# A long single-core network kernel: background steps moved into the down projections, and the S5 outputs set two tiles behind the states

## The chip, the cores and the metric

One core of one Trainium2 chip runs the whole program in one launch. The metric is device time in microseconds (us), lower is better. A difference of 0.2% (4.9 us here) is about the least that a measurement of this kernel can tell from none.

## The reference

The network is two blocks of two layers on 512 tokens of width 1024, all in fp32. Cut to what matters here:

```python
def conv_glu_ffn(h, w_in, conv_w, conv_b, w_out):      # F = 2816, twice (ffn0, ffn1)
    u = h @ w_in
    up = jnp.pad(u, ((0, 0), (CONV_WIDTH - 1, 0), (0, 0)))
    u = sum(conv_w[k] * up[:, k:k + S] for k in range(CONV_WIDTH)) + conv_b
    gate, val = jnp.split(u, 2, axis=-1)
    return (jax.nn.gelu(gate, approximate=True) * val) @ w_out

def _s5_mixer(h, w_in, lam_re, ..., d, w_glu, b_glu):  # once (s5)
    u = (h @ w_in).astype(f32)
    ...                                                # a diagonal state space: 64 groups, 64 states,
    ...                                                # chunks, y = C x + d u
    y = jax.nn.gelu(y); return value * sigmoid(gate)   # of y @ w_glu + b_glu
```

The second block's layers are also scaled and shifted by vectors `silu(cond) @ ada_w + ada_b` (here: the "ada" products, a vector of 1024 times a matrix).

## The kernel before

**Stages.** The body runs pool, ffn0, attention, ffn1, s5, mlp0, ssd, mlp1 and a last norm one after the other; tokens lie on the free axis in two halves of 256. A product of fp32 matrices is three matmuls (`mm3`, L220 to L222): each operand is split in a high and a low part, high by high, low by high, high by low. Weights come in chunks of 512 KB (`wchunk`: a DMA on SP's queue, L192; ScalarE copies the high part, L205; VectorE subtracts the low part, L206). TensorE (PE) has four PSUM banks for products.

**The order.** The program writes the operations in some order, and a scheduler that comes with the tile framework turns this, before the launch, into one fixed queue for each engine. An engine takes its own queue strictly from the front; a row whose data isn't there holds back all rows behind it.

**An ffn layer** (`ffn_layer`, from L960) takes its 22 tiles of F in three phases: 8, 8 and 6. In a phase, each *pair* of tiles is a product of 96 matmuls into four banks (some 22 us), whose results VectorE reads at L969 (`u`, four rows for a pair; they make the banks free for the next pair) before the convolution (L975, L976), the gelu and the split (L321). After the phase, except the last, the *down projection* multiplies by `w_out`, 8 output tiles, each ended by `evac` (L1042). The last pairs' tail and the norm that follows are in `tail_` and the seam to the next layer.

**Background work.** `Background` holds generators; `bg[0](n)` takes n steps of each. It is called after each pair (with `rate`, L1039) and after each evacuation of a down projection (L1043, one step).

- In ffn0 the generator is `s5_tables`, about 72 steps that compute tables for the s5 stage, mostly on VectorE (L681 to L791) with small transposes on PE (L725, L784, L786). Whatever is left is emitted after the body.
- In ffn1 it is `s5_toeplitz` (16 steps: loads `tz`, ScalarE copies `th` at L805) and the ada products of `ada_units` (`vecmat`, L477 to L520), about 60 steps. These make 14 *blocks*. A block takes 8 loads of 256 KB (`as`, L495, two buffers, issued on POOL's queue), each multiplied and added on VectorE into `aa` (L498 for the first, L500 for the next seven; one buffer); ScalarE and VectorE split `aa` into three parts `ab` (L512, L514), and 12 matmuls of one column (`pn`, L484) sum over the partitions. VectorE reads `pn` at L487 (`sums`). One step is two loads, so a block is four steps. `due` puts a block's `pn` and `sums` behind the next block's second load.

**The s5 body** (L1466 to L1507) goes over 8 tiles. `states(n)`: PE forms `pv` (L1394) from the input U and table `vt`; ScalarE and VectorE rotate, scan and rotate back, and leave `xs`, whose first column POOL clears (L1407). `outputs(n)`: PE adds two products with table `ct` into `py` (L1416 from U, L1417 from `xs`; one bank), ScalarE copies it to `ys` and sends it through memory to be regrouped. `gelu(n)` reads that back (`yf`), makes `gh` (ScalarE) and `gl` (POOL, L1431). `glu_mm` multiplies these by `w_glu`. `tabs` and `ctabs` load tables on POOL's queue, 2 MB a tile. `project_u` makes the inputs of two tiles (48 products of mm3's kind); those of tiles 6 and 7 are made in iteration 1.

Of the kernel before, what the change touches and what calls it, by code (L numbers as in the profile page):

```python
# [21 lines left out]
P = 128  # L22
# [3 lines left out]
KD = D // P  # L26
# [36 lines left out]
def net_kernel(ctx: ExitStack, tc: tile.TileContext, I: dict, out: bass.AP, parts=ALL):  # L63
    nc = tc.nc
    V, A, G, T = nc.vector, nc.scalar, nc.gpsimd, nc.tensor
# [12 lines left out]
    def nm(s):  # L78
        uid[0] += 1
        return f"{s}_{uid[0]}"  # L80

    def at(s="a", dt=F32):
        return ap.tile([P, S], dt, tag="a", name=nm(s))
# [7 lines left out]
    def psmm():  # L91
        return psm.tile([P, 512], F32, tag="mm", name=nm("mm"))

    FULL = (0, S)
# [739 lines left out]
    bg = [no_bg]  # L834
# [125 lines left out]
    def ffn_layer(l, phases, late=None, rate=3):  # L960
        win, wout = I["ffn_w_in"][l], I["ffn_w_out"][l]
        S_ = {"ah": [], "al": [], "ft": [], "sq": Norm()}
        hd = Held([(win, 0, KD, c, 0, {}) for c in (0, F1)])
        nk = phases[-1][1] - phases[-1][0]
        tl = Held([(wout, phases[-1][0], nk, n * P, nk % 4, {}) for n in range(0, KD, 2)])

        def scaled(ps):
            u = tt("u")
            V.tensor_tensor(u, ps, S_["pre"].rs, ALU.mult)  # L969
            return u  # L970

        def conv(t, u, col):
            wv = lambda i: vc("ffn_conv_w", 3 * 44 * l + 44 * i + col)
            A.activation(t, u, AF.Identity, bias=vc("ffn_conv_b", 44 * l + col), scale=wv(2))
            V.scalar_tensor_tensor(t[:, 1:], u[:, :S - 1], wv(1), t[:, 1:], ALU.mult, ALU.add)  # L975
            V.scalar_tensor_tensor(t[:, 2:], u[:, :S - 2], wv(0), t[:, 2:], ALU.mult, ALU.add)  # L976

        def glu(j, ug, uv):
            tg, tv = tt("tg"), tt("tv")
            conv(tg, ug, j)  # L980
            A.activation(tg, tg, AF.Gelu_apprx_tanh)
            conv(tv, uv, JF + j)
            V.tensor_tensor(tv, tv, tg, ALU.mult)
            hi, lo = at("hi", F32R), at("lo", F32R)
            S_["split"], _ = split_to(hi, lo, tv, FULL)
            S_["ah"].append(hi)
            S_["al"].append(lo)

        def head(hf, pre):
            S_["pre"] = pre  # L990
            un = S_.setdefault("un", {})

            def evac(i, q, ps, span):
                if hf == 0:
                    un[i, q] = tt("un")
                V.tensor_tensor(un[i, q][:, slice(*span)], ps, pre.rs[:, slice(*span)], ALU.mult)
                if hf and i % 2:
                    glu(i - 1 + q, un.pop((i - 1, q)), un.pop((i, q)))

            hd.run(hf, pre.hi, pre.lo, evac)  # L1000

        def down(n, ps, span, first, last):
            ts = slice(*span)
            ft = S_["ft"]
            if first:
                ft.append(at("f"))
                A.activation(ft[n], ps, AF.Copy)
            else:
                V.tensor_tensor(ft[n][:, ts], ft[n][:, ts], ps, ALU.add)
                if last:  # L1010
                    S_["sq"].add(ft[n], span)

        def body_():
            hh, hl = S_["pre"].hi, S_["pre"].lo
            bg[0](2)
            for ph, (j0, j1) in enumerate(phases):
                final = ph == len(phases) - 1
                if final and late is not None:
                    late()
                for j in range(j0 if ph else 2, j1, 2):  # L1020
                    pp = {(i, q): psmm() for i in range(2) for q in range(2)}
                    src = [chunks(win, 0, KD, i * F1 + j * P) for i in range(2)]
                    if final and j == j1 - 2:
                        chs = [list(c) for c in src]
                        for q in range(2):
                            for i in range(2):
                                for ch in chs[i]:
                                    mm_chunk(pp[i, q], ch, q, hh, hl, KD, FULL)
                        for i in range(len(tl.runs)):
                            tl.load_apart(i)  # L1030
                    else:
                        for _ in range(2):
                            for i in range(2):
                                ch = next(src[i])
                                for q in range(2):
                                    mm_chunk(pp[i, q], ch, q, hh, hl, KD, FULL)
                    for q in range(2):
                        glu(j + q, *(scaled(pp[i, q]) for i in range(2)))
                    bg[0](rate)  # L1039
                if not final:  # L1040
                    def evac(n, ps, span):
                        down(n, ps, span, ph == 0, False)  # L1042
                        bg[0](1)  # L1043

                    project(wout, j0, j1 - j0, 0, (0, 8), S_["ah"], S_["al"], evac)
                    S_["ah"], S_["al"] = [], []

        def tail_(hf, nxt):
            if hf == 0:
                warm_sqrt(S_["split"].ins)  # L1050
            tl.run(hf, S_["ah"], S_["al"], lambda i, q, ps, span: down(2 * i + q, ps, span, False, True))

        return Layer(lambda nxt: PreScale(nxt, eps1, ("ffn_pre_g", 8 * l)), hd.load, head, body_, tail_,
                     lambda span, nxt, pre: post_add(S_["ft"], S_["sq"], "ffn_post_g", 8 * l, span, nxt, pre))

# [286 lines left out]
    def s5_layer(dr, pool, pa):  # L1342
# [43 lines left out]
        def states(n):  # L1386
            cs, sn = rot.pop(n)
            dec = tt("dec")
            G.tensor_copy(g3(dec), dr["r8"][:, 8 * n:8 * n + 8].unsqueeze(2).broadcast_to([P, 8, 64]))
            G.memset(g3(dec)[:, :, 0:1], 0.0)  # L1390
            pv = pa.tile([P, 512], F32, tag="pv", bufs=2, name=nm("pv"))
            for g in range(8):
                w = min(P, 512 - g * 64)
                S_["states"] = T.matmul(pv[:, g * 64:g * 64 + w], vt[n][g // 4][:, (g % 4) * P:(g % 4) * P + P],  # L1394
                                        U[n][:, g * 64:g * 64 + w], start=True, stop=True).ins
            vt.pop(n)
            sw, t1 = swapped(pv), tt("t1")
            V.tensor_tensor(t1, pv, cs, ALU.mult)
            V.tensor_tensor(sw, sw, sn, ALU.mult)
            V.tensor_tensor(t1, t1, sw, ALU.subtract)  # L1400
            st = tt("st")
            V.tensor_tensor_scan(st, dec, t1, 0.0, ALU.mult, ALU.add)
            sw = swapped(st)
            V.tensor_tensor(st, st, cs, ALU.mult)
            V.tensor_tensor(sw, sw, sn, ALU.mult)
            x_ = at("xs")
            G.memset(g3(x_)[:, :, 0:1], 0.0)  # L1407
            V.tensor_tensor(g3(x_)[:, :, 1:], g3(st)[:, :, :63], g3(sw)[:, :, :63], ALU.add)
            xs[n] = x_

# [54 lines left out]
        def body_():  # L1465
# [3 lines left out]
            def project_u(j):  # L1469
# [4 lines left out]
                for q in range(2):  # L1474
                    u_out(j + q, ps[q])

            for j in range(2 * S5_HEAD, KD - 2, 2):
                project_u(j)
            pp = None
            gk = 0  # L1480
            for n in range(KD + 2):
                if n == 1:
                    with tc.issue_after(S_["states"]):
                        project_u(KD - 2)
                    pp = [psmm() for _ in range(4)]
                if n == 2:
                    c0 = [list(chunks(wg, 0, KD, c)) for c in (0, D)]
                if n == 0:
                    stack = ExitStack()
                    for ins in S_["lastu"]:  # L1490
                        stack.enter_context(tc.issue_after(ins))
                if n < KD:
                    states(n)
                    tabs(n + 4)
                    ctabs(n + 1)
                if n == 0:
                    stack.close()
                if 0 <= n - 1 < KD:
                    outputs(n - 1)
                if 0 <= n - 2 < KD:  # L1500
                    gelu(n - 2)
                if n >= 5:
                    with tc.issue_after(S_["last"]):
                        glu_mm(pp, c0, range(gk, n - 4))
                    gk = n - 4
            S_["gk"] = gk
            S_["pp"], S_["c0"] = pp, c0  # L1507

# [461 lines left out]
    for name in names:  # L1970
# [20 lines left out]
            layer.body()  # L1991
            close("atc", "atps")
        elif name == "ffn1":
            layer = ffn_layer(1, ((0, 8), (8, 16), (16, 22)), rate=4)
            seam(prev, layer)
            if tables_due:
                start_tables()
# [75 lines left out]
```

## Time and profile before

| | |
|---|---|
| time, median of 3 runs | 2448.88 us (2448.77, 2448.88, 2451.74) |
| the profiled execution: its own time | 2448.6 us |
| its span, from first to last instruction | 2446.9 us |
| mean granted clock of TensorE | 0.974 of full speed |
| busy: PE / VectorE / ScalarE / POOL | 2303.6 / 1707.1 / 1139.7 / 419.4 us |
| ffn0, its seam to attention | about 36 to 490 us |
| ffn1, its seam to s5 | about 640 to 1130 us |
| s5 body | about 1141 to 1240 us |

Times within the trace are us from the span's start. PE is VectorE's customer and supplier at once: a stage is as fast as PE where PE never waits, and a wait of PE is a direct loss. "PEclk" is the share of the full 2.4 GHz that TensorE was granted, between 0.5 (1.2 GHz) and 1.

### The profile page before, as it was taken

The page shows a single profiled execution, that of the slowest core. Times are in us where ns is not written, and L with a number is a line of the kernel's source. Part 1 is how long each engine was busy: PE and PEld are TensorE (multiplying, and loading weights), DVE is VectorE, ACT ScalarE, POOL GpSimd, SP SyncE. Part 2 cuts the span into 40 slices and gives each one's busy share as a digit, 9 for nine tenths or more (in the row PEclk, how much of TensorE's full clock was granted, in tenths as well). Part 3 has the DMA queues.
Part 4 walks back from the last instruction along what each step waited for, and adds up shares of the span by engine and source line. Part 5 has one row for each costly group of instructions (what it writes and reads, how often), then busy time and mean ns, then how long its engine had stood idle before and what let it go on. Part 6 is the DMA issues. An engine that isn't in the chain of part 4 may idle for free.

```text
span 2446.9 us, 33813 instructions
## 1 busy us (share of the span) xinstructions
PE 2303.6 (94%) x12477; PEld 1948.5 (80%) x12477; DVE 1707.1 (70%) x3064; ACT 1139.7 (47%) x2030; POOL 419.4 (17%) x596
## 2 busy tenths in 40 slices
PE   6989998788989999988799999999999999999998
PEld 6778877775878888787779878789878878888888
DVE  6896979767778697886646666666777788533333
ACT  6533535466675343455534333344555554422322
POOL 2001120002431211110301011010242340200110
PEclk9999999889989999989899999999999999999999
DMA  4224453311465655455742555542333332233322
GB/s 123 81 91 137 145 152 118 106 59 45 127 193 174 195 179 190 159 198 170 220 141 73 172 164 189 186 151 74 113 95 99 108 101 89 91 95 98 100 82 74
DMA packets 265190, 315.52 MB, mean 129 GB/s; under 512 B 34161, under 2 KB 222401, under 8 KB 264001
## 3 DMA queue, kind: packets, MB, share of 16 engines
q1 hardware_dynamic: 220929, 233.64, 30.5%
q0 software_dynamic: 19648, 62.41, 8.1%
q10 hardware_dynamic: 24448, 17.31, 2.2%
q8 instruction: 98, 1.61, 0.3%
q14 instruction: 67, 0.55, 0.1%
HBM read 289.12 MB, written 24.18 MB: 128 GB/s over the span
## 4 chain that ended last, share of the span: by engine, by line
PE 63%; DVE 14%; DMA 10%; issue 7%; ACT 4%; POOL 1%; SPq 0%; ACTq 0%; DVEq 0%; POOLq 0%
PE mm L221 18%; PE mm L220 18%; PE mm L222 18%; DMA as<-in_ada_w 6%; DVE wl L206 3%; DVE aa L500 1%; ACT wh L205 1%; PE pb L1746 1%; PE mm L1676 1%; PE mm L1677 1%; PE mm L1678 1%; DMA tz<-d_k 1%; DVE u L969 1%; PE py L1417 1%; DVE aa L514 1%
## 5 line engine op out<-in xcount | busy, mean ns | idle before, releaser
L220 PE MATMUL mm<-h,wh 128*128 128x512 f32 (+1 forms) x1792 | 665.6, 373 | 31.9 <-ACT h L429 16.2
L221 PE MATMUL mm<-h,wh 128*128 128x512 f32 (+1 forms) x1792 | 666.7, 373 | 7.4 <-DVE h L430 3.7
L222 PE MATMUL mm<-h,wl 128*128 128x512 f32 (+1 forms) x1792 | 663.4, 371 | 0.2 <-DVE wl L206 0.2
L205 ACT ACTIVATE wh<-ws 128x1024 fp32r<-128x1024 f32 (+1 forms) x367 | 387.1, 1059 | 505.6 <-PE mm L221 427.6
L206 DVE TENSOR_TENSOR wl<-ws,wh 128x1024 fp32r<-128x1024 f32 (+1 forms) x367 | 462.3, 1262 | 210.9 <-ACT wh L205 204.5
L220 PEld LDWEIGHTS mm<-h,wh 128*128 128x128 f32 x1792 | 346.2, 194 | 90.5 <-ACT h L429 17.4
L221 PEld LDWEIGHTS mm<-h,wh 128*128 128x128 f32 x1792 | 347.0, 194 | 64.9 <-DVE h L398 5.7
L222 PEld LDWEIGHTS mm<-h,wl 128*128 128x128 f32 x1792 | 346.9, 194 | 55.6 <-issue 1.8
L220 PE MATMUL mm<-hi,wh 128*128 128x512 f32 (+1 forms) x1056 | 371.5, 356 | 10.4 <-ACT wh L205 10.0
L221 PE MATMUL mm<-lo,wh 128*128 128x512 f32 (+1 forms) x1056 | 372.5, 354 | 3.4 <-DVE lo L321 3.0
L222 PE MATMUL mm<-hi,wl 128*128 128x512 f32 (+1 forms) x1056 | 372.1, 354 | 3.1 <-DVE wl L206 3.1
L220 PEld LDWEIGHTS mm<-hi,wh 128*128 128x128 f32 x1056 | 202.0, 192 | 38.4 <-ACT wh L205 11.4
L221 PEld LDWEIGHTS mm<-lo,wh 128*128 128x128 f32 x1056 | 202.2, 191 | 30.4 <-DVE lo L321 4.8
L222 PEld LDWEIGHTS mm<-hi,wl 128*128 128x128 f32 x1056 | 201.8, 191 | 30.1 <-DVE wl L206 4.0
L500 DVE SCALAR_TENSOR_TENSOR aa<-as,cond,aa 128x512 f32<-128x512 f32 x168 | 131.0, 780 | 112.0 <-DMA as<-in_ada_w 110.9
L1298 POOL TENSOR_TENSOR r<-r 128x512 f32<-128x512 f32 x64 | 87.7, 1374 | 670.7 <-ACT r L1294 484.3
L512 ACT ACTIVATE ab<-aa 128x512 bf16<-128x512 f32 x78 | 51.7, 662 | 118.1 <-DVE aa L500 81.1
L321 DVE TENSOR_TENSOR lo<-r,hi 128x512 fp32r<-128x512 f32 x64 | 47.2, 743 | 76.7 <-ACT hi L319 76.6
L495 POOL DMA_DIRECT2D as<-in_ada_w x96 | 51.6, 538 | 241.7 <-DVE aa L500 120.7
L1319 DVE SCALAR_TENSOR_TENSOR x<-mm,mod,x 128x512 f32<-128x512 f32 (+1 forms) x76 | 48.9, 662 | 58.4 <-PE mm L222 58.3
L319 ACT ACTIVATE hi<-r 128x512 fp32r<-128x512 f32 x64 | 40.4, 631 | 71.1 <-POOL r L1298 71.0
L297 DVE TENSOR_TENSOR acc<-acc,sq 128x256 f32<-128x256 f32 (+1 forms) x148 | 62.5, 440 | 9.3 <-ACT sq L296 5.2
(507 smaller groups left out, 3669.0 us busy)
## 6 DMA issues: line engine op xcount, KB each, us to landing
ws<-in_mlp_w SPq DMA_DIRECT2D x124, 512.0 KB, 4.0
ws<-in_ffn_w_in SPq DMA_DIRECT2D x88, 512.0 KB, 4.4
as<-in_ada_w POOLq DMA_DIRECT2D x96, 256.0 KB, 3.2
as<-in_ada_w SPq DMA_DIRECT2D x96, 256.0 KB, 3.4
ws<-in_m_w_in SPq DMA_DIRECT2D x41, 512.0 KB, 3.7
ws<-in_ffn_w_out SPq DMA_DIRECT2D x40, 512.0 KB, 3.4
ws<-in_w_o SPq DMA_DIRECT2D x16, 512.0 KB, 3.9
ct<-d_tab POOLq DMA_DIRECT2D x8, 1024.0 KB, 5.7
```

Source lines behind the costliest of these rows:

```text
L205: A.activation(h_, s_, AF.Copy)
L206: V.tensor_tensor(l_, s_, f(h_), ALU.subtract)
L220: T.matmul(ps, wh, xh, start=first, stop=False)
L221: T.matmul(ps, wh, xl, start=False, stop=False)
L222: return T.matmul(ps, wl, xh, start=False, stop=last).ins
L297: V.tensor_tensor(dst, dst, sq[:, a:b], ALU.add)
L321: return hi_, V.tensor_tensor(lo[:, ts], src, f(hi[:, ts]), ALU.subtract)
L495: queue.dma_start(st, W[k * P:(k + 1) * P, cb * 512:(cb + 1) * 512])
L500: V.scalar_tensor_tensor(acc, st, col(k), acc, ALU.mult, ALU.add)
L512: A.activation(pv[j], av, AF.Copy)
L1298: G.tensor_tensor(r, r, r, ALU.mult)
L1319: V.scalar_tensor_tensor(xT[n][:, ts], ps, md(i, 5, n), xT[n][:, ts], ALU.mult, ALU.add)
```

## The change

In both ffn layers, no background step is taken after the last pair of the last phase, and two are taken at each evacuation of a down projection instead of one. In ffn1 the steps after a pair go from 4 to the default 3 (ffn0 keeps 5). In s5, the outputs run two tiles behind the states instead of one, the gelu three behind instead of two, the glu products start one iteration later; the inputs of tiles 6 and 7 are made in four pieces, one in each of the iterations 1 to 4; a tile's `ct` table is issued after the outputs before it; and `xs` is cleared before `pv` is formed.

```diff
             for q in range(2):
                 glu(j + q, *(scaled(pp[i, q]) for i in range(2)))
-            bg[0](rate)
+            if not (final and j == j1 - 2):
+                bg[0](rate)
         if not final:
             def evac(n, ps, span):
                 down(n, ps, span, ph == 0, False)
-                bg[0](1)
+                bg[0](2)
...
     G.memset(g3(dec)[:, :, 0:1], 0.0)
+    x_ = at("xs")
+    G.memset(g3(x_)[:, :, 0:1], 0.0)
     pv = pa.tile([P, 512], F32, tag="pv", bufs=2, name=nm("pv"))
...
-    x_ = at("xs")
-    G.memset(g3(x_)[:, :, 0:1], 0.0)
     V.tensor_tensor(g3(x_)[:, :, 1:], g3(st)[:, :, :63], g3(sw)[:, :, :63], ALU.add)
...
+    def project_steps(j):
+        ps = [psmm(), psmm()]
+        for i, ch in enumerate(last_w):
+            for q in range(2):
+                mm_chunk(ps[q], ch, q, hh, hl, KD, FULL)
+                if i:
+                    u_out(j + q, ps[q])
+                yield
...
-    for n in range(KD + 2):
+    for n in range(KD + 3):
         if n == 1:
+            last_w = list(chunks(win, 0, KD, (KD - 2) * P, perm=True))
+            last_u = project_steps(KD - 2)
+        if 1 <= n < 5:
             with tc.issue_after(S_["states"]):
-                project_u(KD - 2)
+                next(last_u, None)
+        if n == 5:
             pp = [psmm() for _ in range(4)]
...
             states(n)
             tabs(n + 4)
-            ctabs(n + 1)
...
-        if 0 <= n - 1 < KD:
-            outputs(n - 1)
         if 0 <= n - 2 < KD:
-            gelu(n - 2)
-        if n >= 5:
+            outputs(n - 2)
+        if n:
+            ctabs(n)
+        if 0 <= n - 3 < KD:
+            gelu(n - 3)
+        if n >= 6:
             with tc.issue_after(S_["last"]):
-                glu_mm(pp, c0, range(gk, n - 4))
-            gk = n - 4
+                glu_mm(pp, c0, range(gk, n - 5))
+            gk = n - 5
...
-    layer = ffn_layer(1, ((0, 8), (8, 16), (16, 22)), rate=4)
+    layer = ffn_layer(1, ((0, 8), (8, 16), (16, 22)))
```

The same instructions run; only their places differ. Three places in the engines' queues follow. The numbers behind names count buffers and differ between the two programs.

**Place 1, VectorE, in ffn1, around the first `u` (L969) of the second phase's first pair.** Before, the rows up to its second:

```order
L498 TENSOR_SCALAR aa_8391<-as_8389,cond 128x512
L500 SCALAR_TENSOR_TENSOR aa_8391<-as_8393,cond,aa_8391 128x512
L206 TENSOR_TENSOR wl_8640<-ws_8638,wh_8639 128x1024
L969 TENSOR_TENSOR u_8520<-mm_8396,rsx_7033 128x512
L500 SCALAR_TENSOR_TENSOR aa_8391<-as_8572,cond,aa_8391 128x512
L500 SCALAR_TENSOR_TENSOR aa_8391<-as_8575,cond,aa_8391 128x512
L206 TENSOR_TENSOR wl_8670<-ws_8668,wh_8669 128x1024
L500 SCALAR_TENSOR_TENSOR aa_8391<-as_8578,cond,aa_8391 128x512
L969 TENSOR_TENSOR u_8522<-mm_8398,rsx_7033 128x512
```

With the change:

```order
L498 TENSOR_SCALAR aa_8325<-as_8323,cond 128x512
L487 TENSOR_REDUCE sums_8343<-pn_8330 128x4
L500 SCALAR_TENSOR_TENSOR aa_8325<-as_8327,cond,aa_8325 128x512
L531 TENSOR_TENSOR mod<-sums_8343,vec 128x4
L500 SCALAR_TENSOR_TENSOR aa_8325<-as_8346,cond,aa_8325 128x512
L500 SCALAR_TENSOR_TENSOR aa_8325<-as_8349,cond,aa_8325 128x512
L500 SCALAR_TENSOR_TENSOR aa_8325<-as_8416,cond,aa_8325 128x512
L500 SCALAR_TENSOR_TENSOR aa_8325<-as_8419,cond,aa_8325 128x512
L500 SCALAR_TENSOR_TENSOR aa_8325<-as_8422,cond,aa_8325 128x512
L500 SCALAR_TENSOR_TENSOR aa_8325<-as_8425,cond,aa_8325 128x512
L969 TENSOR_TENSOR u_8590<-mm_8466,rsx_7033 128x512
L969 TENSOR_TENSOR u_8592<-mm_8468,rsx_7033 128x512
```

The pair's first `u` now stands behind all eight loads of the block `aa_8325`, and behind `sums` of the block before it; before, it stood behind two loads of its block. Between the last `u` of the phase before and this one there are now 33 loads (L498 and L500), before 24. At the same place of the third phase there are 35, before 23, and there too all eight loads of a block and a `sums` stand ahead of the `u`.

**Place 2, PE, the same moment: the last rows ahead of the second pair's first matmul (L220).** Before:

```order
L484 LDWEIGHTS ab_8383
L484 MATMUL pn_8556<-one_86,ab_8383 128x1
L484 LDWEIGHTS ab_8383
L484 MATMUL pn_8556<-one_86,ab_8383 128x1
L220 MATMUL mm_8604<-h_6596,wh_8609 128x512
L221 MATMUL mm_8604<-h_6597,wh_8609 128x512
```

With the change:

```order
L484 LDWEIGHTS ab_8317
L484 MATMUL pn_8330<-one_86,ab_8317 128x1
L484 LDWEIGHTS ab_8430
L484 MATMUL pn_8444<-one_86,ab_8430 128x1
L484 LDWEIGHTS ab_8430
L484 MATMUL pn_8444<-one_86,ab_8430 128x1
L484 LDWEIGHTS ab_8430
L484 MATMUL pn_8444<-one_86,ab_8430 128x1
L484 LDWEIGHTS ab_8430
L484 MATMUL pn_8444<-one_86,ab_8430 128x1
L220 MATMUL mm_8652<-h_6596,wh_8657 128x512
L221 MATMUL mm_8652<-h_6597,wh_8657 128x512
```

Before, twelve `pn` matmuls stood between the two pairs, all of the block `aa_8211`, which was finished in the rows ahead. Now there are sixteen: the twelve of `pn_8330`, which place 1's `sums` waits for and which stand behind the whole first pair, and four on `ab_8430`, which is made from `aa_8325` when its eighth load has been added. `mm_8652` needs the bank that the first `u` frees.

**Place 3, POOL, in s5, around the first `gl` (L1431 before, L1432 with the change).** `xs_11482` before is tile 3's, and so is `xs_11407` with the change. Before:

```order
L1361 DMA ct_11493<-d_tab 128x2048
L1389 COPY dec_11522<-r_103 128x512
L1390 MEMSET dec_11522 128x8
L1431 TENSOR_TENSOR gl_11453<-yf_11449,gh_11452 128x512
L1407 MEMSET xs_11482 128x8
L1353 DMA vt_11485<-d_tab 128x512
```

With the change:

```order
L1393 MEMSET xs_11407 128x8
L1354 DMA vt_11433<-d_tab 128x512
L1354 DMA vt_11434<-d_tab 128x512
L1391 MEMSET dec_11489 128x8
L1362 DMA ct_11538<-d_tab 128x2048
L1390 COPY dec_11551<-r_103 128x512
L1432 TENSOR_TENSOR gl_11467<-yf_11463,gh_11466 128x512
L1391 MEMSET dec_11551 128x8
L1393 MEMSET xs_11492 128x8
```

Tile 3's clearing moves from behind the first `gl` to ahead of it; tile 4's (`xs_11492`) is now the first one behind it.

## Rows read from the trace of the kernel before

**Rows 1.** The page, part 1: busy time, share of the span, instructions.

```profile
PE 2303.6 (94%) x12477; PEld 1948.5 (80%) x12477; DVE 1707.1 (70%) x3064; ACT 1139.7 (47%) x2030; POOL 419.4 (17%) x596
```

**Rows 2.** The chain that ended last, 780 to 1090 us: its shares by line.

```profile
by line: DMA as<-in_ada_w 29.3%; issue 25.3%; DVE aa L500 6.9%; DVE wl L206 6.5%; DVE u L969 3.0%; PE mm L221 2.7%; ACT wh L205 2.6%; DVE tg L975 2.4%; PE mm L222 2.3%; PE mm L220 2.2%; DVE aa L514 1.9%; DVE tv L975 1.9%; POOL as L495 1.6%;
```

**Rows 3.** VectorE in order of time: start, duration, line, operation [idle before, releaser].

```profile
790.70 0.68 DVE L969 TENSOR_TENSOR u<-mm,rsx 128x512 f32<-128x512 f32 x1
...
810.60 0.49 DVE L498 TENSOR_SCALAR aa<-as,cond 128x512 f32<-128x512 f32 x1 [0.70 <-ACT ab L512]
...
838.88 0.75 DVE L500 SCALAR_TENSOR_TENSOR aa<-as,cond,aa 128x512 f32<-128x512 f32 x1 [2.26 <-DMA as<-in_ada_w]
...
843.10 0.75 DVE L500 SCALAR_TENSOR_TENSOR aa<-as,cond,aa 128x512 f32<-128x512 f32 x1 [1.67 <-DMA as<-in_ada_w]
...
850.74 0.49 DVE L498 TENSOR_SCALAR aa<-as,cond 128x512 f32<-128x512 f32 x1 [0.70 <-ACT ab L512]
...
853.07 0.68 DVE L969 TENSOR_TENSOR u<-mm,rsx 128x512 f32<-128x512 f32 x1
```

**Rows 4.** The same view, start of the third phase.

```profile
926.99 0.68 DVE L969 TENSOR_TENSOR u<-mm,rsx 128x512 f32<-128x512 f32 x1
...
948.47 0.47 DVE L498 TENSOR_SCALAR aa<-as,cond 128x512 f32<-128x512 f32 x1
...
991.83 0.49 DVE L498 TENSOR_SCALAR aa<-as,cond 128x512 f32<-128x512 f32 x1 [0.70 <-ACT ab L512]
```

**Rows 5.** TensorE in order of time: a wait in ffn0, two ends of first pairs.

```profile
137.95 0.77 PE L220 MATMUL mm<-h,wh 128*128 128x512 f32 x1 [6.06 <-DVE u L969]
...
857.02 0.45 PE L484 MATMUL pn<-one,ab 128*128 128x1 bf16 x12
...
991.22 0.35 PE L484 MATMUL pn<-one,ab 128*128 128x1 bf16 x8
```

**Rows 6.** DMA issues: count, KB each, median us from issue to landing.

```profile
as<-in_ada_w POOLq DMA_DIRECT2D x96, 256.0 KB, 3.2
```

**Rows 7.** Groups by line, VectorE, 30 to 475 us: first and last of 20 table lines.

```profile
L763 DVE TENSOR_TENSOR ct<-b,s5v 128x512 f32<-128x512 f32 x16 | 11.0, 685 | 0.1
...
L689 DVE MEMSET s5z<- 128x128 f32 x1 | 0.2, 165 | 0.0
```

**Rows 8.** Stretches: PE, PEld, DVE, ACT, POOL busy (instructions), PEclk, DMA share, GB/s.

```profile
138.00:148.00 10.00, 10.00 (x36) 8.08 (x37) 10.00 (x27) 5.29 (x8) 0.00 (x0) 0.80 0.01 2
190.00:230.00 40.00, 40.00 (x195) 32.62 (x194) 20.59 (x33) 13.21 (x18) 6.00 (x10) 1.00 0.43 132
340.00:370.00 30.00, 30.00 (x142) 24.25 (x141) 17.30 (x31) 7.73 (x10) 5.97 (x40) 1.00 0.47 145
410.00:440.00 30.00, 20.34 (x119) 16.51 (x117) 29.77 (x53) 14.96 (x23) 3.46 (x6) 0.77 0.57 179
1030.00:1050.00 20.00, 14.62 (x79) 12.54 (x78) 19.14 (x26) 11.65 (x16) 1.61 (x3) 0.83 0.66 218
1160.00:1220.00 60.00, 47.42 (x319) 44.56 (x318) 39.81 (x47) 30.91 (x46) 19.29 (x36) 0.89 0.74 233
```

**Rows 9.** Waits of TensorE, 1070 to 1130 us: total, times, longest.

```profile
PE mm L220 <- ACT h L429: 6.1, 2, 4.2
PE pn L314 <- DVE dg L311: 4.0, 2, 3.0
...
PE pn L484 <- ACT ab L512: 1.2, 2, 0.7
```

**Rows 10.** The same view, the s5 body, 1141 to 1240 us.

```profile
PE py L1417 <- DVE xs L1408: 5.6, 3, 4.0
PE py L1417 <- POOL xs L1407: 2.5, 1, 2.5
PE py L1416 <- ACT ys L1420: 2.4, 2, 1.7
...
PE pv L1394 <- DVE t L1398: 1.9, 1, 1.9
```

## The prediction, made blind

> **What bounds the kernel now.** I read the page first: PE is busy 94% of the span, VectorE 70% [rows 1]. So only two things can change the time by much: waits of PE, and stretches in which it runs below full clock. I then listed PE's waits by stretch, the clock in the same stretches, and last the chain that ended last, to see who is late. Two stretches lose to VectorE's table work and the clock that falls after it (410 to 440), to the end of the ada steps (1030 to 1050); s5 loses in a string of waits [rows 8, 10]. But the chain of waits says something that PE's own waits do not: from 780 to 1090 the largest part of the chain that ended last, 29%, is the landing of `as` loads, and VectorE's adding of them is the next work on it [rows 2]. PE hardly waits there, but the row of loads has no slack. The change puts more of them into that stretch.
>
> **The pace of the loads.** `as` has two buffers, so a load waits until VectorE has finished with the load two before it. From 810.60 to 850.74, through the down projection, VectorE went through two blocks, 16 loads: 40.14 / 16 = 2.51 us a load, and stood idle for the DMA between them [rows 3]. In the third phase two blocks took 948.47 to 991.83: 2.71 us a load [rows 4]. The quickest two in succession came 4.22 us apart, 2.11 each [rows 3].
>
> **ffn1: what is added.** Eight evacuations ask for 2 steps of 2 loads each, 32 loads in a down projection and more with the pairs. VectorE's queue keeps that order: between the last `u` of the first phase and the first `u` of the second there are now 33 loads, before 24. From 790.70, 33 x 2.51 = 82.8 us end at 873.5. PE ends the first pair at 857.0 [rows 3, 5], and cannot begin the second: it needs that `u` for the bank, and has `pn` matmuls of the unfinished block ahead in its own queue. It waits **16 us**. Before, the `u` came at 853.07, in time. At the third phase there are 35 loads: from 926.99, 87.9 us end at 1014.8, and the pair ends at 991.2 [rows 4, 5]: **24 us**, both shifted alike by the first wait. Behind the `u` on VectorE stand the convolution and the weights' low parts; PE stands, so they cost nothing beyond that. The pairs after it have 8 loads or fewer each, 20 us in a pair of 22: no further wait.
>
> Bounds. At 2.71 us a load the waits are 23 and 31. At 2.11 the sum of loads gives 3 and 10, but a second rule of the order holds then: `sums` ahead of the last seven loads needs `pn` matmuls that stand behind the whole first pair. Of those seven, two lie in the buffers; five at 2.11 and two additions of 0.75 [rows 3] make 12 us after the pair's end, at each place. So 24 to 54, and I take 40, from the pace of the down projection that these loads run in.
>
> One rule of the skill would make it less. The median landing of these loads is 3.2 us for 256 KB [rows 6]. The Trainium skill (DMA: Bandwidth & Descriptors, section Anatomy of one DMA — SWDGE (gpsimd) path) gives 2.0 us plus the bytes at 436 GB/s for a load of this kind, an estimate of 2.6 us here; with two in flight that takes 0.3 us off the pace of 2.51, and the waits would be 12 and 13 instead of 16 and 24. The trace shows the longer landing, beside the weight loads of the same stretch, and no run here shows the shorter; the sum goes by the trace.
>
> **The clock after a wait.** After a wait of 6.06 us in ffn0, the next 10 us, in which PE was busy throughout, were granted 0.80 [rows 5, 8]: 2 us lost. Two waits, 2 us each: **4 us**; at most 3 each, since 1030 to 1050 with its waits lost 0.17 x 14.6 = 2.5 us [rows 8].
>
> **ffn0: what is moved.** 120 us of table work on VectorE [rows 7] over some 72 steps are 1.67 us a step. The 8 extra steps in each down projection are 13.3 us, put where VectorE was free 19.4 of 40 us (190 to 230) and 12.7 of 30 (340 to 370) [rows 8]: no wait of PE. These steps are VectorE's own work with few loads, so they have no pace but VectorE's. At the end, 9 steps fewer (10 for 15 and 4 leftovers) take 15 us off VectorE where it is busy 29.77 of 30 us; PE lost there 30 - 20.3 = 9.7 us waiting and 0.23 x 20.3 = 4.7 us by the clock, 14.4 in all [rows 8]. Some of it is weights that land late, so I take **-11**, between -4 (the work merely moves to the start of a phase) and -14.
>
> **ffn1's end and the seam.** No ada step is left there. 1030 to 1050 lost 5.4 us waiting and 2.5 by the clock [rows 8]: -8. In the seam the waits on `ab` (1.2), on `h` (6.1) and on `dg` (4.0) [rows 9] stand in part behind the last block's splits on ScalarE and VectorE; they also exist in a seam without such work, so -6 of 11. Together **-14**, between -5 and -19. The last block's loads leave POOL's queue to the s5 tables there; that is in it.
>
> **s5.** The same work with one tile more between states and outputs, and the last input products cut in four, so that a tile's `pv` can come between them; that moves work on PE and saves none. Waits on `xs`, its clearing, `ys` and `t`: 12.4 us, and the clock 0.11 x 47.4 = 5.2: 17.6 at most [rows 10, 8]. Sure is the clearing, 2.5, which no longer stands behind `gl`. The rest hangs on whether the chain of a tile on ScalarE and VectorE, or the transfers (0.74 of the DMA engines over 60 us [rows 8]), set the pace anyway; the loads that read tiles 6 and 7 back now come later too, behind a `yf` on SP's queue. **-6**, between 0 and -18.
>
> **The sum**, on the profiled execution's 2448.6 (its span is 2446.9; the median of the runs, 2448.88, is 0.3 above): 40 + 4 - 11 - 14 - 6 = +13, so **2462 us**. What counts as no change is 0.2%, 4.9 us.
>
> **Rivals.**
> - *The loads come quickly* (the other side). The mechanism is the pace of `as`: the waits are 68p - 130.6 for a pace p, and with the clock they equal the gains of 31 at p = 2.32. Below that the floor of 24 holds: 24 + 4 - 31 = -3, 2446; with gains of 40, 2437. For it: VectorE waits for the DMA, not for work, and two loads came at 2.11. Against: no whole block ran below 2.5.
> - *The gains don't come* (s5 stays bound by its transfers and a tile's chain, table work comes back at the start of ffn0's phases): gains of 9, so 2484; with the pace of 2.71 as well 2497. For it: the DMA share in s5, and VectorE nearly full in ffn0.
> - *All gains come in full*, the waits as forecast: 44 - 51 = -7, 2442. Against: it needs every clock loss to go.
>
> **How the numbers follow.** The forecast, waits of 35 to 54 with gains of 20 to 35, has 0.62: 2452 to 2475 or so, slower. The second rival has 0.16, slower. The first has 0.17, a little more than half of it within 4.9 us of before; the third 0.05, faster. Faster 0.12, the same 0.13, slower 0.75. The range of 2444 to 2482 leaves a tenth on either side.
>
> **What would show it.** In the changed profile: two waits of PE of over 10 us, just after the first pair of ffn1's second and third phases (near 857 and, shifted, 1007), put down to `ab` or `u`, with a granted clock below 1 behind each; VectorE idle on `as` there; 410 to 440 and the end of ffn1 free of waits over 1 us; no wait on POOL's clearing in s5. It is wrong if PE goes from pair to pair there without a stop, or if the waits are under 10 us, and then 68p - 130.6 has failed.

## The result, and the profile after

| | before | changed |
|---|---|---|
| time, median | 2450.31 us (4 runs, 2448.77 to 2456.92) | 2475.85 us (4 runs, 2473.06 to 2481.46) |
| ratio of the times | | 1.0102, 95% interval 1.0076 to 1.0128 |
| the profiled execution: its own time, span | 2448.6, 2446.9 | 2476.7, 2475.0 |
| mean granted clock | 0.974 | 0.969 |

Slower by 25.5 us, 1.0%. Forecast was 2462, in a range of 2444 to 2482. PE does the same work:

```profile
PE 2300.2 (93%) x12477; PEld 1942.5 (78%) x12477; DVE 1714.8 (69%) x3064; ACT 1142.9 (46%) x2030; POOL 418.4 (17%) x596
```

PE's 2300.2 us answer to the 2303.6 of before [rows 1]; the added time is waiting. To see where, four moments that both traces have: PE's first matmul of attention's part that waits for `kr`, a norm's product at the start of ffn1, the first input product of s5, and s5's first product behind `sgm`. The changed kernel, TensorE in order of time:

```profile
496.89 0.80 PE L220 MATMUL mm<-h,wh 128*128 128x512 f32 x1 [2.44 <-DVE kr L1113]
...
694.44 0.68 PE L314 MATMUL pn<-dg,ones 128*128 128x128 f32 x4 [0.89 <-DVE dg L311]
...
1152.44 0.79 PE L220 MATMUL mm<-h,wh 128*128 128x512 f32 x1 [2.54 <-DVE us L1370]
...
1265.05 0.50 PE L220 MATMUL mm<-gh,wh 128*128 128x512 f32 x1 [2.02 <-ACT sgm L1460]
```

And the kernel before (the numbers in brackets are the idle time just before a row and what ended it):

```profile
521.97 0.79 PE L220 MATMUL mm<-h,wh 128*128 128x512 f32 x1 [2.44 <-DVE kr L1112]
...
720.76 1.19 PE L314 MATMUL pn<-dg,ones 128*128 128x128 f32 x4 [4.70 <-DVE dg L311]
...
1128.79 0.79 PE L220 MATMUL mm<-h,wh 128*128 128x512 f32 x1 [2.01 <-DVE us L1369]
...
1239.87 0.50 PE L220 MATMUL mm<-gh,wh 128*128 128x512 f32 x1 [2.00 <-ACT sgm L1459]
```

Attention is reached **25.1 us earlier** (496.89 for 521.97), ffn1 26.3 earlier, s5's first product **23.7 later**, so ffn1 costs **+50.0**; s5 ends 25.2 later (+1.5), and the span ends 28.1 later (some 3 us in the stages behind, in small pieces). So the small loss is the difference of a gain and a loss that are both large. (Such a moment differs by a few us between executions: three kernels whose ffn0 is as before reach the `kr` wait at 521.97, 523.86 and 526.10.)

The two waits are there. TensorE's waits from 826 to 856 us, the start of the second phase:

```profile
PE pn L484 <- ACT ab L512: 21.2, 4, 16.1
```

and from 975 to 1020, the start of the third (0.7 us more stand earlier, in the pair):

```profile
PE pn L484 <- ACT ab L512: 26.7, 7, 14.9
```

VectorE in order of time shows what they wait for:

```profile
764.79 0.68 DVE L969 TENSOR_TENSOR u<-mm,rsx 128x512 f32<-128x512 f32 x1
...
835.28 0.48 DVE L498 TENSOR_SCALAR aa<-as,cond 128x512 f32<-128x512 f32 x1
835.67 0.16 DVE L487 TENSOR_REDUCE sums<-pn 128x4 f32<-128x12 f32 x1
...
839.68 0.75 DVE L500 SCALAR_TENSOR_TENSOR aa<-as,cond,aa 128x512 f32<-128x512 f32 x1 [3.06 <-DMA as<-in_ada_w]
...
849.56 0.75 DVE L500 SCALAR_TENSOR_TENSOR aa<-as,cond,aa 128x512 f32<-128x512 f32 x1 [0.66 <-DMA as<-in_ada_w]
850.23 1.28 DVE L969 TENSOR_TENSOR u<-mm,rsx 128x512 f32<-128x512 f32 x2
...
924.78 0.68 DVE L969 TENSOR_TENSOR u<-mm,rsx 128x512 f32<-128x512 f32 x1
...
1016.45 1.28 DVE L969 TENSOR_TENSOR u<-mm,rsx 128x512 f32<-128x512 f32 x2
```

From the first phase's last `u` (764.79) to the next one (850.23) VectorE spent 85.4 us on 33 loads, 2.59 us each, and from 924.78 to 1016.45 91.7 us on 35, 2.62 each. In front of many loads it stands idle for the landing, 3.06 us in the longest case shown. PE had ended the first pair's product at 829.0 and the third phase's first pair at 993.2. These rows answer to [rows 3, 4].

The changed kernel by stretches (columns as in [rows 8]):

```profile
410.00:450.00 40.00, 39.01 (x272) 36.28 (x271) 27.46 (x50) 19.21 (x34) 0.00 (x0) 1.00 0.35 105
450.00:500.00 50.00, 41.27 (x305) 39.47 (x305) 44.04 (x122) 31.41 (x82) 0.00 (x0) 0.91 0.26 80
831.50:851.50 20.00, 1.25 (x17) 1.00 (x18) 9.56 (x16) 3.52 (x6) 4.73 (x9) 0.52 0.45 145
852.00:862.00 10.00, 10.00 (x43) 7.68 (x43) 9.61 (x18) 5.25 (x8) 1.07 (x2) 0.79 0.16 50
1018.00:1028.00 10.00, 10.00 (x39) 7.68 (x40) 9.92 (x17) 6.04 (x9) 0.54 (x1) 0.73 0.15 47
```

The first two rows are ffn0's end and the seam behind it: 39.0 of 40 us busy at full clock in the first. The third is the wait, PE busy 1.25 of 20 us; the fourth and fifth are the 10 us behind each wait, at 0.79 and 0.73, PE busy throughout: 2.1 and 2.7 us lost.

In s5 PE's waits on `xs` and its clearing [rows 10] are gone, and one on `ys` has come. Waits of TensorE, 1164 to 1270 us:

```profile
PE py L1417 <- ACT ys L1421: 15.0, 5, 5.3
```

### The profile page after: what moved, and what is told of

Read it like the earlier page. It is cut to its first block, busy times and chain, and to the rows that moved or that the text cites. A ratio compares the mean times of both kernels' runs of the same rounds, so it can differ in the third digit from the quotient of the medians.

```text
span 2475.0 us, 33840 instructions
## 1 busy us (share of the span) xinstructions
PE 2300.2 (93%) x12477; PEld 1942.5 (78%) x12477; DVE 1714.8 (69%) x3064; ACT 1142.9 (46%) x2030; POOL 418.4 (17%) x596
## 4 chain that ended last, share of the span: by engine, by line
PE 43%; DVE 5%; DMA 2%; ACT 1%; issue 1%; DVEq 0%; ACTq 0%
PE mm L221 12%; PE mm L220 12%; PE mm L222 12%; DMA as<-in_ada_w 2%; DVE wl L206 1%; PE pb L1762 1%; PE mm L1692 1%; PE mm L1693 1%; PE mm L1694 1%; DVE aa L500 0%; ACT wh L205 0%; DVE u L394 0%; PE pb L1768 0%; DMA ws<-in_mlp_w 0%; PE py L1417 0%
## 5 line engine op out<-in xcount | busy, mean ns | idle before, releaser
L220 PE MATMUL mm<-h,wh 128*128 128x512 f32 (+1 forms) x1792 | 665.0, 373 | 23.5 <-ACT h L429 7.3
L220 PEld LDWEIGHTS mm<-h,wh 128*128 128x128 f32 x1792 | 344.7, 193 | 81.6 <-issue 8.8
L220 PE MATMUL mm<-hi,wh 128*128 128x512 f32 (+1 forms) x1056 | 369.1, 354 | 6.8 <-ACT wh L205 6.1
L220 PEld LDWEIGHTS mm<-hi,wh 128*128 128x128 f32 x1056 | 200.7, 190 | 34.2 <-ACT wh L205 6.8
L500 DVE SCALAR_TENSOR_TENSOR aa<-as,cond,aa 128x512 f32<-128x512 f32 x168 | 130.9, 779 | 132.3 <-DMA as<-in_ada_w 131.1
L495 POOL DMA_DIRECT2D as<-in_ada_w x96 | 51.6, 538 | 252.5 <-DVE aa L500 120.2
```

The lines of the kernel that those rows point to most:

```text
L220: T.matmul(ps, wh, xh, start=first, stop=False)
L495: queue.dma_start(st, W[k * P:(k + 1) * P, cb * 512:(cb + 1) * 512])
L500: V.scalar_tensor_tensor(acc, st, col(k), acc, ALU.mult, ALU.add)
```

## The experiments

**The three parts by themselves.** Each edit alone in the kernel before. A ratio is always to the kernel before as measured beside the run; its median was 2452.05, 2450.65 or 2448.18 us, so runs that stand far apart below are best compared by their ratios. First ffn0:

```diff
-                    bg[0](rate)
+                    if not (l == 0 and final and j == j1 - 2):
+                        bg[0](rate)
...
-                        bg[0](1)
+                        bg[0](1 if l else 2)
```

> The kernel before with the change in ffn0 alone: two table steps at each evacuation, none after the last pair; ffn1 and s5 as before. Theory (the change gains 25 us in ffn0 and its seam and loses 50 in ffn1): the trace of the changed kernel reaches attention's first product 25 us earlier, so 2424 us, with everything behind it moved by the same 25. Rival (the earlier start only moves a wait into attention or ffn1, and the gain is given back there): 2440 or above.

Measured: 2427.58 us (before: 2452.05), ratio 0.9900, interval 0.9877 to 0.9923. The theory holds: 24.5 us, and no more of it is given back behind than the runs' spread. The stretches of this run:

```profile
410.00:450.00 40.00, 38.77 (x261) 35.60 (x260) 28.50 (x50) 20.25 (x35) 0.00 (x0) 1.00 0.31 99
450.00:500.00 50.00, 41.21 (x322) 39.84 (x320) 42.31 (x121) 29.06 (x77) 0.00 (x0) 0.94 0.25 79
```

and the same of the kernel before, to the wait for `kr` (at 499.87 above, at 521.97 here):

```profile
410.00:450.00 40.00, 28.50 (x183) 24.32 (x182) 35.47 (x65) 18.62 (x29) 5.33 (x9) 0.83 0.51 165
450.00:522.10 72.10, 57.07 (x423) 54.38 (x421) 51.17 (x142) 36.46 (x96) 0.45 (x2) 0.87 0.22 68
```

Idle time is 11.5 + 15.0 us before, 1.2 + 8.8 now: 16.5 less. The half clock cost 0.17 x 28.5 + 0.13 x 57.1 = 12.3 us before, 0.06 x 41.2 = 2.5 now: 9.8 less. So more than a third of what went is clock, and half of the clock's part lies in the seam, behind 450. (The two make 26.3, more than the 22.1 us by which this trace reaches `kr` earlier: at 410 the two programs are not at quite the same work. The shares are rough.)

Then ffn1 alone (two steps at an evacuation and none after the last pair where `l` is 1, `rate` 3):

```diff
-                    bg[0](rate)
+                    if not (l == 1 and final and j == j1 - 2):
+                        bg[0](rate)
...
-                        bg[0](1)
+                        bg[0](2 if l else 1)
...
-            layer = ffn_layer(1, ((0, 8), (8, 16), (16, 22)), rate=4)
+            layer = ffn_layer(1, ((0, 8), (8, 16), (16, 22)))
```

> The kernel before with the change in ffn1 alone: two ada steps at each evacuation, three after a pair, none after the last. Theory (two waits behind the as loads, 21 and 27 us, and 5 us of half clock, little gained at the end): 2449 + 50 = 2499 us, two waits of over 15 us each in the phases' first pairs. Rival (part of the two waits came from attention ending earlier, so that loads and weights collided): under 2485.

Measured: 2503.61, ratio 1.0219, interval 1.0200 to 1.0237: 51.6 us slower. Waits of TensorE in this run, 856 to 886 us, and then 1005 to 1050:

```profile
PE pn L484 <- ACT ab L512: 21.0, 4, 15.7
```

```profile
PE pn L484 <- ACT ab L512: 26.3, 6, 15.4
```

They have the size that they have in the whole change, so they owe nothing to attention's earlier end. And s5 alone, the s5 part of the diff, of which this is a piece:

```diff
-            for n in range(KD + 2):
+            for n in range(KD + 3):
...
-                if 0 <= n - 1 < KD:
-                    outputs(n - 1)
...
+                    outputs(n - 2)
...
```

> The kernel before with the change in s5 alone. Theory (the waits on xs and its clearing go, waits of the same size on ys come in their place, since py has one bank and its copy stands on ScalarE behind the state chain of the tile in work): 2450, within 4 us of before. Rival (what I forecast: the waits go by half): 2443.

Measured: 2450.73, ratio 1.0003, interval 0.9992 to 1.0013: no difference. The waits of TensorE in its s5 body, 1141 to 1242 us, where before there were 12.4 us [rows 10]:

```profile
PE py L1416 <- ACT ys L1420: 14.1, 4, 7.1
```

One wait has taken the other's place. The three parts add up: -24.5 + 51.6 - 1.3 = +25.8, and the whole change measured +25.5.

**What sets the pace of the loads.** The whole change, with more `as` buffers; `tz` gives up one, to make room:

```diff
-                st = pool.tile([P, 512], F32, tag="as", bufs=2, name=nm("as"))
+                st = pool.tile([P, 512], F32, tag="as", bufs=4, name=nm("as"))
...
-            tz = pool.tile([P, 8, P], F32, tag="tz", bufs=2, name=nm("tz"))
+            tz = pool.tile([P, 8, P], F32, tag="tz", bufs=1, name=nm("tz"))
```

> The whole change with four as buffers instead of two, and one tz buffer instead of two to make room. Theory (the pace of 2.5 us a load is the round trip of two buffers, landing plus VectorE plus issue): four in flight bring the pace toward 1.3 us, 33 loads end in time, both waits fall under 5 us and the time to about 2430. Rival (the pace is set by the issuing engine or by the bandwidth beside the weight loads): the two waits stay over 15 us each, and the time at 2470 to 2480.

Measured: 2423.95, ratio 0.9891, interval 0.9873 to 0.9909: 51.9 us under the whole change. Both waits are gone (the view lists no wait of TensorE from 780 to 1010). VectorE in this run, the first rows of two blocks with two blocks' loads from one to the other:

```profile
794.02 0.48 DVE L498 TENSOR_SCALAR aa<-as,cond 128x512 f32<-128x512 f32 x1
...
819.91 0.49 DVE L498 TENSOR_SCALAR aa<-as,cond 128x512 f32<-128x512 f32 x1 [0.70 <-ACT ab L512]
```

25.9 us for 16 loads, 1.62 each, for 2.51 [rows 3], though a load takes longer to land than the 3.2 us of before [rows 6]:

```profile
as<-in_ada_w POOLq DMA_DIRECT2D x96, 256.0 KB, 3.6
```

Three buffers, the same edit with `bufs=3`:

> The whole change with three as buffers and one tz buffer. Theory (the pace is the round trip divided by the buffers): 5.0 us by 3 is 1.7 us a load, 32 loads take 54 us where PE gives 66, so both waits are gone, or nearly, and the time is that of four buffers, 2424 to 2432. Rival (a fixed time per load sets it): waits of 10 us or more stay.

Measured: 2427.75, ratio 0.9904, interval 0.9885 to 0.9924. Of the two waits 2.7 and 3.6 us are left. The same two rows:

```profile
797.05 0.49 DVE L498 TENSOR_SCALAR aa<-as,cond 128x512 f32<-128x512 f32 x1 [0.70 <-ACT ab L512]
...
828.59 0.49 DVE L498 TENSOR_SCALAR aa<-as,cond 128x512 f32<-128x512 f32 x1 [0.70 <-ACT ab L512]
```

1.97 us a load. So 2, 3 and 4 buffers give 2.51, 1.97 and 1.62: the buffers in flight set the pace, but less than in proportion (pace times buffers is 5.0, 5.9, 6.5 us). The landing grows a little, and the waits for it run out: of the two blocks' time VectorE waited 14.2 us for landings with two buffers, 7.6 with three and 2.1 with four, where it was busy for 19.0 of the 25.9 us. With four, VectorE's own work and the splits at a block's end are most of the pace. Nor are three buffers as good as four, though the medians differ by 3.8 us only: in the profiled executions ffn1, from its first product to s5's, takes 432.9 us with three and 419.9 with four. The control, one `tz` buffer with two of `as`:

> The whole change with one tz buffer and as as it is, two. It tells what the smaller tz alone does in the runs with more as buffers. Theory: nothing that matters, 2470 to 2480 with the two waits of 21 and 27 us. Rival (part of the gain with four buffers came from tz): under 2460.

Measured: 2475.38 in one run, with waits of 22.3 and 24.4 us on `ab`. The smaller `tz` does nothing that one run can tell.

**Fewer steps in ffn1's down projections.** The whole change (three steps after a pair, none after the last), with

```diff
-                        bg[0](2)
+                        bg[0](1 if l else 2)
```

> The whole change, but in ffn1 one ada step at each evacuation as before (three after a pair, none after the last). Theory (the two steps make the lateness; with one there are 23 loads in each stretch and no wait, but three blocks are left for the end and the seam): no wait over 2 us at the phases' starts, 5 to 15 us lost at the seam, 2430 to 2440. Rival (the waits come from the place of sums and pn behind the pair, not from the number of loads): waits of 10 us stay.

Measured: 2460.18, ratio 1.0038, interval 1.0023 to 1.0054. The first half of the theory holds: PE waits 0.2 us in all for a `u`, and for no `ab`, at the phases' starts, with 23 loads ahead of each first `u`. The time is 20 us over what I expected. Three blocks are left for the end, and PE waits for them there, from 1045 to 1092 us:

```profile
PE pn L484 <- ACT ab L512: 36.1, 6, 15.0
```

36.1 us, on the last two of the three: what is left over does not slip in between the seam's work, it stands ahead of it in PE's queue in one heap, at the pace of two buffers. The loads' lateness can be put in two places, but with two buffers this edit does not schedule it away. The kernel before does, with four steps after every pair, the last too: there PE waits 2.4 us for `ab` in all of ffn1.

**What holds s5.** In the changed kernel ScalarE shows why `ys` is late (ScalarE in order of time):

```profile
1210.63 0.59 ACT L1384 ACTIVATE sw<-pv 64x512 f32<-64x512 f32 x1
1215.81 0.63 ACT L1383 ACTIVATE sw<-st 64x512 f32<-64x512 f32 x1 [4.59 <-DVE st L1405]
1216.45 0.63 ACT L1384 ACTIVATE sw<-st 64x512 f32<-64x512 f32 x1
1217.11 0.60 ACT L1421 ACTIVATE ys<-py 128x512 f32<-128x512 f32 x1
```

The copy of `py` to `ys`, which frees the one `py` bank, stands behind the two swaps of the next tile's state, and in every tile these wait for VectorE's scan, 4.59 us here and 30.2 us in the eight tiles. An edit on the kernel with four `as` buffers takes the outputs between the scan and the swaps:

```diff
             V.tensor_tensor_scan(st, dec, t1, 0.0, ALU.mult, ALU.add)
+            if n >= 2:
+                outputs(n - 2)
             sw = swapped(st)
...
-                if 0 <= n - 2 < KD:
+                if KD <= n < KD + 2:
                     outputs(n - 2)
```

> The kernel with four as buffers, and in s5 the outputs of two tiles back taken between the scan and the rotation back, so that the copy of py to ys stands on ScalarE ahead of the two swaps that wait for the scan. Theory (s5 gains nothing because that copy waits behind the scan of another tile, 4 us a tile, and py has one bank): the five waits on ys, 15 us in all, fall under 5, and the time drops by 8 to 12 from 2424, to 2412 to 2416. Rival (s5 is bound by its table transfers or a tile's chain on VectorE): PE waits as long for something else, and the time stays within 4 us of 2424.

Measured: **2409.09 us**, ratio 0.9828, interval 0.9812 to 0.9845, 14.9 under the run without the edit (15.4 by the ratios), more than expected. TensorE's waits in its s5 body, 1110 to 1212 us:

```profile
PE py L1419 <- ACT ys L1423: 5.0, 2, 3.3
PE mm L220 <- ACT sgm L1462: 2.0, 1, 2.0
PE py L1420 <- POOL xs L1393: 1.1, 1, 1.1
```

15 us on `ys` have become 5.0. Is the two tiles' distance needed for it? The same kernel, with outputs one tile behind again:

```diff
-            if n >= 2:
-                outputs(n - 2)
+            if n >= 1:
+                outputs(n - 1)
...
-                if n:
-                    ctabs(n)
-                if 0 <= n - 3 < KD:
-                    gelu(n - 3)
-                if n >= 6:
+                ctabs(n + 1)
+                if 0 <= n - 2 < KD:
+                    gelu(n - 2)
+                if n >= 5:
...
```

> The kernel of the run with four as buffers and the early copy of py, but with the outputs one tile behind the states again, the gelu two behind and the glu products one iteration earlier, as before the change; the input products stay in four pieces. Theory (what s5 needs is the copy ahead of the swaps, and the second tile of distance is what lets py be formed while the scan of the next tile runs, with nothing waiting on xs): waits on xs come back, 5 us or more, and the time is 4 to 10 above 2409. Rival (the distance is worth nothing once the copy comes early): within 3 us of 2409.

Measured: 2421.5, ratio 0.9891, interval 0.9874 to 0.9908: 12.4 above (15.4 by the ratios). Waits in its s5 body, 1110 to 1225 us:

```profile
PE py L1420 <- DVE xs L1411: 12.2, 6, 3.1
```

So the distance takes the wait off `xs`, and the earlier copy takes it off `ys`; each alone only changes the name of the wait. The length of s5 in the traces, from its first input product to the product behind `sgm`, says the same: 110.3 to 111.1 us in the three kernels with s5 as before, 109.2 to 113.6 in the five with the change as it is, 112.9 here with the early copy but one tile's distance, and 100.4 with both.

**ffn1 as before, with the rest.** The early copy and the change in ffn0 and s5; ffn1 with two buffers, one step, `rate` 4:

```diff
-                    if not (final and j == j1 - 2):
+                    if not (l == 0 and final and j == j1 - 2):
...
-                        bg[0](2)
+                        bg[0](1 if l else 2)
...
-            layer = ffn_layer(1, ((0, 8), (8, 16), (16, 22)))
+            layer = ffn_layer(1, ((0, 8), (8, 16), (16, 22)), rate=4)
```

> The change in ffn0 and in s5 with the early copy of py; ffn1 as before, with two as buffers, one ada step at an evacuation, four after a pair. Theory (in ffn1 the earlier ada steps gain little at the end even without their waits, 3 us of the 14 that I forecast): 2427.6 less the 15 of s5, 2413, 2 to 5 above the run with four buffers. Rival (the end of ffn1 gains 14 once the loads come in time): 2420 or above.

Measured: 2417.65 (2410.52 to 2419.7), ratio 0.9870, interval 0.9846 to 0.9895, so 8.6 above the run with four buffers (10.3 by the ratios): over the 2 to 5 expected and under the rival's 2420. The intervals nearly touch. Part of the miss is s5: against the run with ffn0's part alone (2427.58) the distance and the early copy gave 9.9 us here (7.4 by the ratios), not the 15 that I had put in. Where s5's first product starts, in this run and in the one with four buffers and the early copy:

```profile
1106.49 0.80 PE L220 MATMUL mm<-h,wh 128*128 128x512 f32 x1 [2.15 <-DVE us L1370]
```

```profile
1101.75 0.79 PE L220 MATMUL mm<-h,wh 128*128 128x512 f32 x1 [2.02 <-DVE us L1370]
```

Up to there the two differ by 4.7 us: this run is 0.7 later at ffn1's first product (681.77 for 681.05) and takes 4.0 longer from it to s5's. The other 4 lie in s5 (101.9 for 100.4) and behind it, and are not explained.

## Why the prediction was right in kind and half in size

The direction and the mechanism of the loss were right, and the time lies in the range, near its end; the forecast change was +13 and the measured one +25.5. That the total came out no further off is partly luck: ffn0 was 13.5 us too small a gain, ffn1's end and s5 together 15.3 too large, and the two misses nearly cancel. Nor do the forecast's own bounds add up to its "2452 to 2475": waits of 35 to 54 with gains of 20 to 35 and the clock make 2453 to 2487. Term by term, in us:

| term | forecast | measured |
|---|---|---|
| the two waits for the `as` loads | +40 (16 + 24) | +48.6 (21.2 + 27.4) |
| the clock in the 10 us behind each | +4 | +4.8 |
| ffn0's end and seam | -11 | -24.5 |
| ffn1's end and its seam | -14 | about -3, by subtraction |
| s5 | -6 | -1.3 |

**The waits.** *PE waits at the first pairs of two phases, since 33 and 35 loads stand ahead of a `u`.* Shown three ways: the part alone makes them, more buffers take them away, and fewer loads take them away. The loads came a little slower, 2.59 and 2.62 us each for the 2.51 that I took. The first wait is 5 us longer than forecast: 2.6 by this pace, and 2.1 since the pair ended 64.2 us after the last `u` and not 66.3. In the second, PE stood from the pair's end at 993.2 to the `u` at 1016.45, 23.3 us for the 24 forecast, and 3.7 more inside the pair, for the late `pn` of an earlier block; that part I did not have. (In the first 5 us of the one wait and the first 9 of the other PE stands at the `pn` of the block before; the `u` comes later than that, so they add nothing.) My quickest pace, 2.11, was misread by a little: the loads from 819.39 to 823.54 took 2.08 each. The lower bound of 24 was the floor's, so it does not move. The Trainium skill (DMA: Bandwidth & Descriptors, section Anatomy of one DMA — SWDGE (gpsimd) path) gives 2.6 us by estimate for one such load, and the waits would have been 25. The traces do not agree: beside the weight loads the medians are 3.2 us with two buffers, 3.5 with three and 3.6 with four. The rival of quick loads, which needed a pace under 2.32, falls by the 2.59 and 2.62.

**The clock** came as forecast, 2.1 and 2.7 for 2 each.

**ffn0.** *"At the end, 9 steps fewer take 15 us off VectorE"*: right, but I priced 410 to 440 only, 14.4 us, and took 11. The loss went on in the seam: PE was idle there for 15.0 us and the clock was 0.87 from 450 to 522, where the run with this part alone has 8.8 us and 0.94. Little of this is table work itself (VectorE has 3.2 us of it behind 450); that the waits and the clock at the end of ffn0 carry into the seam is what the two traces suggest, and no run parts them. I had read the seam's waits for ffn1 and not for ffn0. That is the largest miss, 13.5 us, and it is a stretch that I left out of the sum, not a price.

**ffn1's end.** *"No ada step is left there"* is so, but the waits stayed, and the sign that I had named, no wait over 1 us at ffn1's end, did not come. Waits of TensorE from 1058 to 1160 us:

```profile
PE mm L220 <- ACT wh L205: 6.1, 2, 5.3
PE pn L314 <- DVE dg L311: 4.0, 2, 3.0
PE mm L221 <- DVE h L430: 3.3, 3, 2.0
...
PE mm L220 <- ACT h L429: 1.8, 1, 1.8
```

The first is on a weight copy, and ScalarE in turn waited for the weights' landing:

```profile
1069.63 1.06 ACT L205 ACTIVATE wh<-ws 128x1024 fp32r<-128x1024 f32 x1 [2.66 <-DMA ws<-in_ffn_w_out]
```

The kernel before has the same wait in the stretch that I priced at 5.4 us [rows 8]. Waits of TensorE there, 1030 to 1050, and ScalarE in order of time:

```profile
PE mm L220 <- ACT wh L205: 4.4, 1, 4.4
```

```profile
1038.36 0.63 ACT L205 ACTIVATE wh<-ws 128x512 fp32r<-128x512 f32 x1 [4.38 <-DMA ws<-in_ffn_w_out]
```

So most of those 5.4 us were not the ada steps', and the trace of before could have told me. `dg` waits 4.0 as before [rows 9], without an ada block in front of it, so it was not theirs either. Of the 14 only the waits on `ab` and most of one on `h` went (1.8 for 6.1), and one on `h`'s low part grew (3.3 for 1.3): ffn1's 50.0 less the waits 48.6 and the clock 4.8 leave -3.4. Without the two waits it is worth a little more: from ffn1's first product to s5's the three runs with four buffers take 419.1 to 420.7 us, the four kernels with ffn1 as before 424.7 to 427.7.

**s5.** *"Sure is the clearing"*: that wait went, and the others on `xs` too. I had the rival, that the gains do not come, but by the transfers; what took their place was the copy of `py` in ScalarE's queue, which I had not looked for. The run with the early copy shows that the transfers did not set the pace: it moves the same tables in an s5 of 100.4 us for 113.6.

The net of these misses: 8.6 and 0.8 more loss, 13.5 more gain in ffn0, 15.3 less gain in the last two; 13 + 8.6 + 0.8 - 13.5 + 10.6 + 4.7 = 24.2, where the parts alone gave 25.8.

## What to carry to other kernels

Work that fills idle time has a pace of its own. Ask for each piece what sets it: table work took as many steps as VectorE had room for and gained 24.5 us, while the same two steps per evacuation of loads with two buffers cost 51.6, since a queue taken in order made the main work wait for the landing. Two more buffers took that loss away. And when a wait is moved away, read the queue for who holds the next resource: in s5 neither the distance nor the earlier copy was worth anything alone; together they gave 15 us on the kernel with four buffers and 10 on the one with ffn1 as before. The best version here is the whole change with four buffers and the early copy: 2409.09 us, 1.7% under the kernel before.

## What the runs showed that I had not expected

- The clock was more than a third of ffn0's gain: 16.5 us of idle time went, and some 9.8 us that PE had lost by running at a granted 0.83 to 0.87 around it.
- Three blocks left over cost 36.1 us at the end of ffn1, three quarters of what the two waits cost in the whole change (48.6): VectorE's loads at the pace of two buffers, and PE behind them.
- From two to four buffers the time of a load fell from 2.51 to 1.62 us while its landing grew from 3.2 to 3.6; the DMA engines' busy share over the two blocks went from 0.62 to 0.79, so they had room beside the weights.
